# A diffusion block on one core: the first up-projection weights split ahead of the norms, modulation columns paced anew, a PSUM bank for each output of a last block

## The chip, the cores and the metric

The kernel runs on one core of one Trainium2 chip. The metric is the device time of one execution in microseconds (us); it is the median of several runs. The profile is of one further execution, whose own time stands in the table below.

## The reference, cut to what matters

The program is a backbone of two layers over 256 latent tokens and 256 context tokens, of width 2048, in fp32.

- Layer 0: the conditioning vectors give six modulation vectors (shift, scale, gate, twice) by a 2048 x 12288 product. The normalised, modulated tokens go through one input projection into query latents (512), key/value latents (256), a rotary key (64) and a pooling input (1024). The latents are normalised again and projected up to 8 heads (queries 128 + 64 rotary, keys 128 + the shared rotary key, values 128). The latent tokens attend to context and latent tokens. The pooling input goes through centred means of four widths and a small product. Attention and pooling outputs are concatenated into one output projection, with a gated residual. Then an MLP of 8192 hidden channels with a squared ReLU, again modulated, normalised and gated.
- Layer 1: modulated tokens go through a two-dimensional Fourier transform in 4 channel groups, an output projection with a gated residual, and an MLP as before.
- At the end there is a last RMS norm with its own weight.

```
p = h @ w_in
q = rmsnorm(p[:, :512], q_norm) @ w_uq
kv = rmsnorm(p[:, 512:768], kv_norm) @ w_ukv
x = x + g1 * (concat(attend(q, kv), pool(p[:, 832:])) @ w_out)
x = x + g2 * (square(relu(modulate(rmsnorm(x), sh2, sc2) @ w_mlp1)) @ w_mlp2)
```

## The kernel before, in words

**Precision.** Every large fp32 operand is split into a high part (a cast to fp32r on ScalarE, ACT) and a low part (the difference, on VectorE, DVE); TensorE (PE) multiplies high by high, high by low and low by high. `split` (L131) does this for 128 x 1024 elements of a weight tile, into a tile of tag H and one of tag L, six of each (L52). A weight tile W is 128 x 2048 (1 MB), comes in by one DMA on SyncE (SP) in `load` (L121), and has six buffers (L51). PSUM has eight banks (L57).

**Modulation columns.** For the vectors of layer 0 behind the first two, and for all of layer 1, each 128 columns of the modulation weight are one W tile: DVE multiplies it with the broadcast conditioning and sums it, in one instruction (L103). These tiles wait in a list `todo`. `load` adds `pace[0]` to a counter for each weight that it loads and lets as many columns follow on SP as the counter has whole ones; their sums are issued with the next load (`mod_sums`). `mod_rest` issues what is left. In the mixer of layer 0, 48 columns (gate, scale and shift: `mod_vector(0, 2)`, `(0, 4)`, `(0, 3)`) are due before the MLP's norm.

**Order.** SP and PE run in the order of the program text (`manual_schedule`, L49); the instructions of ACT and DVE are put in an order by the compiler's list scheduler, which mostly keeps the text's and may pull ready work forward. All queues are in order when they run.

**The stages around the change.** A loop over 8 groups computes modulation of the first norm, the latents and the first half of the pooling input. Then `weave(attention(), pooling())` (L725) interleaves two generators: when `attention` yields n, n half steps of `pooling` run on PE before it goes on.

- `attention` (L580): squares of the latents, token sums, `rstd` and `spread` (yield 1, yield 1), the normalised latents and their splits, the shared key's rotary part and its split (yield 2), then `project(0)` for the first pair of heads (yield 1), `scores` (yield 2), and for each head `turned` (transposes of the softmax), for odd heads `project` of the next pair (yield 1), `scores` of the next head, `values`, yield 2. `project` loads and splits the pair's key/value weight (512 KB, one split) and query weight (768 KB, two splits) itself.
- `pooling` (L525): four weight tiles of the second half of the pooling input, in two half steps each; copies out of PSUM with a yield of their own; the band matmuls, the small product, and then the pooling half of the output projection in 16 half steps. 29 half steps in all.

When both are done, four `linear` calls (L728) do the attention half of the output projection in eight loads, `mod_rest` runs, and `renorm` (L300) forms the norm of the MLP; its waking matmuls (`awake`, tile `wk`) keep PE busy meanwhile.

**Output blocks.** `linear` (L183) accumulates four output blocks of 128 channels at a time. With `slim`, two blocks share a bank, each a half of it, and they are evacuated together when the second is done. With `drain`, both half steps of the last weight are done block by block. Both are set in the last group of four of the even projection, of each MLP and of the odd projection. The evacuation is `residual` (L500): a gated update of x on DVE, its square on ACT, and the sum of squares on DVE, for the last two blocks (LATE) left to PE. The very last MLP also scales x by the final norm's weight (L521).

Lines that the prediction's steps touch: L103 column sum, L135 and L136 split, L242 sum of squares, L268 waking matmuls, L512 update, L519 and L521 late square and final scaling, L638 to L644 rotary query, L675 row maximum of the scores, L691 and L694 transposes and their copies.

Of the kernel before, what the change touches and what calls it, by code (L numbers as in the profile page):

```python
# [19 lines left out]
NB = D // P  # L20
# [23 lines left out]
def hybrid_dit(ctx: ExitStack, tc: tile.TileContext, xT, ctxT, c2, cb_in, vecs, wmod_s, wmod0, wmod1,  # L44
# [32 lines left out]
    def half(b, i):  # L77
        return b[:, i * T:(i + 1) * T]
# [42 lines left out]
    def load(src, n=2048):  # L121
        mod_sums()
        w = wp.tile([P, 2048], F32, name="W", tag="W")
        nc.sync.dma_start(w[:, :n], src)
        pace[1] += pace[0]
        while pace[1] >= 1 and todo:
            pace[1] -= 1
            mod_step()
        return w
# [13 lines left out]
    def split_pair(h, l, src):  # L143
        nc.scalar.copy(h, src)
        nc.vector.tensor_tensor(l, src, h.bitcast(F32), ALU.subtract)
# [21 lines left out]
    def narrow(o, wts, j, acts, first, last):  # L167

        js = slice(j * P, (j + 1) * P)
        n = len(wts)  # L170
        for k, (h, l) in enumerate(wts):
            mm(o, h[:, js], acts[k][:, :T], first and k == 0, False)
            mm(o, h[:, js], acts[k][:, T:], False, False)
            mm(o, l[:, js], acts[k][:, :T], False, last and k == n - 1)
# [8 lines left out]
    def linear(tiles, acts, evac, nb=4, slim=False, drain=False):  # L183


        if slim:
            banks = [bank() for _ in range(nb // 2)]
            ps = [half(banks[j // 2], j % 2) for j in range(nb)]
        else:
            ps = [bank() for _ in range(nb)]  # L190
        for i, (srcs, k0) in enumerate(tiles):
            for s, src in enumerate(srcs):
                w = load(src)
                final = i == len(tiles) - 1
                for k in (0, 2):
                    wts = split(w, k * 512, 1024, 512)
                    first, last = i == 0 and k == 0, final and k == 2
                    part = acts[k0 + k:k0 + k + 2]
                    if drain and final:
                        if k == 0:  # L200
                            held = wts
                            yield
                            continue
                        wts, part = held + wts, acts[k0:k0 + 4]
                    elif not slim:
                        wides(ps[4 * s:4 * s + 4], wts, part, first, last,
                              lambda j: evac(4 * s + j, ps[4 * s + j]))
                        yield
                        continue
                    for j in range(4):  # L210
                        o = ps[4 * s + j]
                        if slim:
                            narrow(o, wts, j, part, first and j % 2 == 0, last and j % 2 == 1)
                        else:
                            wide(o, wts, j, part, first, last)

                        if last and not slim:
                            evac(4 * s + j, o)
                        elif last and j % 2:
                            evac(4 * s + j - 1, ps[4 * s + j - 1])  # L220
                            evac(4 * s + j, o)
                    yield
# [108 lines left out]
    def column(i):  # L331
        return vec[:, i:i + 1]
# [153 lines left out]
    ropet = funit("ropet")  # L486
    nc.sync.dma_start(ropet.rearrange("p (a b) -> p a b", b=T), rope)
    bandt = [funit(f"band{i}") for i in range(4)]
    for i in range(4):
        nc.sync.dma_start(bandt[i], band[:, i])  # L490

    mod_vector(0, 2)
    mod_vector(0, 4, V_N2[0])
    mod_vector(0, 3)
    pace[0] = 1.75


    mixed = []
# [1 line left out]
    def residual(l, which, stats, slim=False):  # L500

        def at(ng):
            def evac(j, ps):
                i = 4 * ng + j
                if (l, which) not in whole:
                    mod_sums()
                assert (l, which) in whole
                g = mods[l][:, which, i:i + 1]
                if not slim:
                    t = scr("rt")  # L510
                    nc.scalar.mul(t, half(ps, 1), g)  # L511
                nc.vector.scalar_tensor_tensor(x[:, i], ps[:, :T], g, x[:, i], ALU.mult, ALU.add)  # L512
                if not slim:
                    nc.vector.tensor_tensor(x[:, i], x[:, i], t, ALU.add)  # L514
                if stats is not None and i < NB - LATE:
                    sumsq(stats[0], x[:, i], i == 0)
                elif stats is not None:
                    stats.append(scr("late"))
                    nc.scalar.square(stats[-1], x[:, i])  # L519
                if stats is not None and (l, which) == (1, 5):  # L520
                    nc.scalar.mul(x[:, i], x[:, i], column(V_FN + i))  # L521
            return evac
        return at

    def pooling():  # L525

        ut = [[funit("ut") for hf in range(2)] for tb in range(2)]
        for tb in range(2):
            nc.scalar.copy(ut[tb][0], pu0[tb])
        us = [bank(f"pu{tb}") for tb in range(2)]  # L530
        for kt in range(4):
            w = load(w_pl[1, kt])
            for i in range(2):
                for n, (h, l) in enumerate(split(w, 1024 * i, 1024, 512)):
                    by_token(us, 4 * kt + 2 * i + n, h, l)
                yield
        for tb in range(2):
            nc.scalar.copy(ut[tb][1], us[tb])
        yield
        pooled = []  # L540
        for g in range(4):
            ps = bank("pl")
            for j in range(2):
                fs = slice((g % 2) * T + j * P, (g % 2) * T + (j + 1) * P)
                for tb in range(2):
                    mm(half(ps, j), ut[tb][g // 2][:, fs], half(bandt[g], tb), j == 0 and tb == 0, j == 1 and tb == 1)
            pooled.append(funit("pl"))
            nc.scalar.copy(pooled[g], ps)
            if g % 2:
                yield  # L550
        w = load(w_pool)
        for g in range(4):
            ps = bank("po")
            for j in range(2):
                plain(half(ps, j), [w[:, k * 256:(k + 1) * 256] for k in (2 * g, 2 * g + 1)], j,
                      [half(pooled[g], 0), half(pooled[g], 1)], j == 0, j == 1)
            for j in range(2):
                u = unit("mx")
                sc, o = column(V_PS + 2 * g + j), half(ps, j)
                nc.scalar.mul(u[:, :T], o, sc)  # L560
                nc.vector.scalar_tensor_tensor(u[:, T:], o, sc, u.bitcast(F32)[:, :T], ALU.mult, ALU.subtract)
                mixed.append(u)
            if g % 2:
                yield
        for ng in range(4):
            yield from linear([((w_oe[ng, kt],), 4 * kt - 8) for kt in (2, 3)], mixed,
                              residual(0, 2, None, True)(ng), 4, True)

# [3 lines left out]
    def rotary(s):  # L572

        r = scr("rot")
        nc.vector.stream_shuffle(r, s, list(range(16, 32)) + list(range(16)))
        nc.vector.tensor_tensor(s, s, half(ropet, 0), ALU.mult)
        nc.vector.tensor_tensor(r, r, half(ropet, 1), ALU.mult)
        nc.vector.tensor_tensor(s, s, r, ALU.add)

    def attention():  # L580
        squares = []
        for b in ka[:2] + qa:
            squares.append(funit("lq"))
# [26 lines left out]
            split_act(ql[j], f)  # L610
        kr = funit("kr")
        nc.scalar.copy(kr, ka[2])
        rotary(half(kr, 1))
        krh, krl = unit("krh"), unit("krl")
        split_pair(krh, krl, kr)
        yield 2

        def project(pr):

            w = load(w_ukv[pr], 1024)  # L620
            wkv = split(w, 0, 1024, 512)
            kn, vt = [], []
            for j in range(2):
                js = slice(j * P, (j + 1) * P)
# [5 lines left out]
                    mm(ps, l[:, js], kvh[k], False, k == 1)  # L630
                kn.append((unit("knh"), unit("knl")))
                split_pair(*kn[j], ps)
            w = load(w_uq[pr], 1536)
            wuq = split(w, 0, 768, 384) + split(w, 768, 768, 384)
            ps = bank("qr")
            narrow(half(ps, 0), wuq, 2, ql, True, True)
            f = scr("qr")
# [67 lines left out]
            split_act(a, o)  # L705
            attn.append(a)

        pair = project(0)
        yield 1
        p = scores((pair, 0))  # L710
        yield 2
        for h in range(NH):
            us = turned(p)
            head = (pair, h % 2)
            if h < NH - 1:
                if h % 2:
                    pair = project(h // 2 + 1)
                    yield 1
                p = scores((pair, (h + 1) % 2))
            else:  # L720
                yield 1
            values(head, us)
            yield 2
# [160 lines left out]
    mod_vector(1, 5)  # L884
    acc = [stat("acc3")]
    mlp(1, h, acc, ((9, 0.0), (999, 1.7)))
    r = spread(rstd_of(acc))
    for i in range(0, NB, 2):
        o = funit("o").rearrange("p (a b) -> p a b", b=T)
        nc.vector.tensor_tensor(o, x[:, i:i + 2], r[:, None, :].to_broadcast([P, 2, T]), ALU.mult)  # L890
# [90 lines left out]
```

## Time and profile before

| | before |
|---|---|
| median of 3 runs | 1984.27 us (1983.85 to 1984.52) |
| the profiled execution | 1986.23 us |
| its span, first to last instruction | 1984.5 us |
| PE matmul busy | 1932.1 us, 97% |
| PE weight loads busy | 1707.2 us, 86% |
| DVE busy | 1459.6 us, 74% |
| ACT busy | 1016.6 us, 51% |
| mean granted TensorE clock | 0.991 of full speed |
| column sums, L103 | 160, 364.8 us of DVE |

A share over the whole span averages stages with different limits, so the rows below are of stretches. Times in them are in us from the start of the span. The row of a window gives its length, then the busy time and the count of instructions of each engine, the granted clock as a share of full speed, the busy share of the 16 DMA engines and their GB/s. A row of the timeline gives start, duration, engine, line, operation, output tile and input tiles, shape and count, and in brackets the idle time of the engine just before with what ended it. PEld is the weight load of PE. SPq is the SP queue that issues DMAs; a long duration there is a wait for a buffer.

### The profile page before, as it was taken

The page shows a single profiled execution, that of the slowest core. Times are in us where ns is not written, and L with a number is a line of the kernel's source. Part 1 is how long each engine was busy: PE and PEld are TensorE (multiplying, and loading weights), DVE is VectorE, ACT ScalarE, POOL GpSimd, SP SyncE. Part 2 cuts the span into 40 slices and gives each one's busy share as a digit, 9 for nine tenths or more (in the row PEclk, how much of TensorE's full clock was granted, in tenths as well). Part 3 has the DMA queues.
Part 4 walks back from the last instruction along what each step waited for, and adds up shares of the span by engine and source line. Part 5 has one row for each costly group of instructions (what it writes and reads, how often), then busy time and mean ns, then how long its engine had stood idle before and what let it go on. Part 6 is the DMA issues. An engine that isn't in the chain of part 4 may idle for free.

```text
span 1984.5 us, 29715 instructions
## 1 busy us (share of the span) xinstructions
PE 1932.1 (97%) x11886; PEld 1707.2 (86%) x11886; DVE 1459.6 (74%) x2042; ACT 1016.6 (51%) x1655; POOL 1.2 (0%) x13
## 2 busy tenths in 40 slices
PE   5997999999999999999999999999999999999997
PEld 4786899988888888888888989888888888888887
DVE  4448999998888888888888677897655555555564
ACT  4344654455545644644554454555456446545663
POOL 0000000000000000000000000000000000000000
PEclk9998999999999999999999999999999999999998
DMA  9997899879889879888888347598555555555541
GB/s 379 394 391 256 323 347 348 332 269 371 317 332 345 325 309 345 327 336 315 312 323 318 128 168 260 199 382 306 189 186 185 187 190 190 191 191 191 186 155 43
DMA packets 77468, 537.72 MB, mean 271 GB/s; under 512 B 8849, under 2 KB 9105, under 8 KB 14481
## 3 DMA queue, kind: packets, MB, share of 16 engines
q1 hardware_dynamic: 77328, 535.82, 72.8%
q8 instruction: 93, 1.52, 0.3%
q14 instruction: 47, 0.38, 0.1%
HBM read 533.69 MB, written 2.10 MB: 270 GB/s over the span
## 4 chain that ended last, share of the span: by engine, by line
PE 93%; DVE 4%; DMA 1%; issue 1%; ACT 1%; SPq 0%; DVEq 0%; ACTq 0%
PE mm L81 81%; PE ka L81 2%; DVE W L103 2%; PE mrow L81 2%; PE pu L81 1%; PE f L81 1%; PE qa L81 1%; PE sc L81 1%; DVE L L136 1%; DMA W<-in_wmod_s 1%; PE pv L81 1%; PE p L81 1%; PE var L81 0%; PE wk L81 0%; PE pl L81 0%
## 5 line engine op out<-in xcount | busy, mean ns | idle before, releaser
L136 DVE TENSOR_TENSOR L<-W,H 128x1024 fp32r<-128x1024 f32 (+1 forms) x620 | 743.3, 1214 | 331.8 <-ACT H L135 331.1
L135 ACT CAST H<-W 128x1024 fp32r<-128x1024 f32 (+1 forms) x620 | 638.1, 1044 | 519.3 <-PE mm L81 472.6
L81 PE MATMUL mm<-hid,H 128*128 128x512 f32 (+1 forms) x2176 | 526.9, 379 | 0.0
L81 PE MATMUL mm<-h,H 128*128 128x512 f32 x2048 | 513.2, 392 | 0.0
L81 PEld LDWEIGHTS mm<-hid,H 128*128 128x128 f32 x2176 | 385.3, 189 | 61.7
L81 PEld LDWEIGHTS mm<-h,H 128*128 128x128 f32 x2048 | 368.3, 189 | 66.8 <-DVE h L292 0.5
L103 DVE SCALAR_TENSOR_TENSOR W<-W,cb 128x2048 f32<-128x2048 f32 x160 | 364.8, 2282 | 0.3 <-DMA W<-in_wmod 0.3
L81 PE MATMUL mm<-hid,L 128*128 128x256 f32 x2048 | 303.9, 282 | 0.0
L81 PEld LDWEIGHTS mm<-hid,L 128*128 128x128 f32 x2048 | 286.5, 190 | 18.7
L81 PEld LDWEIGHTS mm<-h,L 128*128 128x128 f32 x2048 | 279.4, 190 | 19.9
L81 PE MATMUL mm<-h,L 128*128 128x256 f32 x2048 | 285.6, 282 | 0.0
L512 DVE SCALAR_TENSOR_TENSOR x<-mm,mods,x 128x256 f32<-128x256 f32 x176 | 78.2, 476 | 51.4 <-ACT rt L511 31.2
L511 ACT ACTIVATE rt<-mm,mods 128x256 f32<-128x256 f32 x132 | 53.9, 470 | 64.1 <-PE mm L81 64.1
L747 ACT COPY b<-mm 128x256 f32<-128x256 f32 x128 | 45.8, 358 | 69.7 <-PE mm L81 69.7
L750 ACT ACTIVATE rl<-g 128x256 f32<-128x256 f32 x128 | 53.2, 416 | 54.5 <-DVE g L748 53.3
L748 DVE TENSOR_TENSOR g<-mm,b 128x256 f32<-128x256 f32 x128 | 53.5, 418 | 25.9 <-ACT b L747 25.7
L81 PE MATMUL mm<-fr,H 128*128 128x512 f32 (+1 forms) x320 | 71.2, 349 | 0.0
L81 PEld LDWEIGHTS mm<-fr,H 128*128 128x128 f32 x320 | 54.5, 190 | 6.2
L751 ACT ACTIVATE hd<-rl 128x256 f32<-128x256 f32 x128 | 53.3, 416 | 2.5
L141 DVE TENSOR_TENSOR hid<-hd,hid 128x256 fp32r<-128x256 f32 x128 | 53.6, 419 | 0.3
L140 ACT CAST hid<-hd 128x256 fp32r<-128x256 f32 x128 | 52.2, 407 | 1.0
L514 DVE TENSOR_TENSOR x<-x,rt 128x256 f32<-128x256 f32 x132 | 50.9, 417 | 0.7
(223 smaller groups left out, 1558.1 us busy)
## 6 DMA issues: line engine op xcount, KB each, us to landing
W<-in_w SPq DMA_DIRECT2D x256, 1024.0 KB, 5.3
W<-in_wmod SPq DMA_DIRECT2D x160, 1024.0 KB, 6.2
W<-in_wmod_s SPq DMA_DIRECT2D x32, 1024.0 KB, 9.6
W<-in_w_oe SPq DMA_DIRECT2D x16, 1024.0 KB, 6.7
W<-in_w_oo SPq DMA_DIRECT2D x16, 1024.0 KB, 5.0
W<-in_w_pl SPq DMA_DIRECT2D x8, 1024.0 KB, 8.4
W<-in_w_kq SPq DMA_DIRECT2D x8, 896.0 KB, 9.2
W<-in_w_uq SPq DMA_DIRECT2D x4, 768.0 KB, 4.6
```

Source lines behind the costliest of these rows:

```text
L81: nc.tensor.matmul(o, l, r, start=start, stop=stop, skip_group_check=True)
L103: nc.vector.scalar_tensor_tensor(w, w, 1.0, cb, ALU.mult, ALU.mult, accum_out=mods[l][:, which, j:j + 1])
L135: nc.scalar.copy(h[:, :n], w[:, lo:lo + n])
L136: nc.vector.tensor_tensor(l[:, :n], w[:, lo:lo + n], h.bitcast(F32)[:, :n], ALU.subtract)
L140: nc.scalar.copy(u[:, :n], src)
L141: nc.vector.tensor_tensor(u[:, n:2 * n], src, u.bitcast(F32)[:, :n], ALU.subtract)
L511: nc.scalar.mul(t, half(ps, 1), g)
L512: nc.vector.scalar_tensor_tensor(x[:, i], ps[:, :T], g, x[:, i], ALU.mult, ALU.add)
L514: nc.vector.tensor_tensor(x[:, i], x[:, i], t, ALU.add)
L748: nc.vector.tensor_tensor(s, half(ps, 0), b, ALU.add)
L750: nc.scalar.activation(r, s, AF.Relu)
L751: nc.scalar.square(f, r)
```

## The change

- **Early weights.** A new function `pair_weights` loads and splits both weights of a pair of heads. For the first pair it is called at the start of `attention`, ahead of the squares and norms; for the others at the start of an odd head, ahead of `turned`. `project` takes the split tiles from a list.
- **Rotary key behind the projection.** The rotary part of the shared key and its split are issued behind `project(0)`.
- **Yields.** After each `project`, 2 half steps of the filler run instead of 1; the yield of its own behind the copies in `pooling` is gone.
- **Bands.** The four 256 KB loads of the band tables are issued one by one behind the four pooling weights instead of ahead of the weave.
- **Paces.** 1.75 columns for each load from the first load on become none for the first three loads (the pair's weights and the first pooling weight), 2.2 from there to the first group of four of the pooling half's output projection, and 1.6 from its second group on.
- **A bank for each last block.** Where `slim` and `drain` are both set, each of the four outputs gets its own bank and is evacuated at once when its matmuls end.
- **Final scaling.** For the last two blocks the scaling by the final norm's weight is issued behind the last norm's `rstd_of`.

```
-        if slim:
+        own = slim and drain
+        if own:
+            ps = [half(bank(), 0) for _ in range(nb)]
+        elif slim:
...
-                            narrow(o, wts, j, part, first and j % 2 == 0, last and j % 2 == 1)
+                            narrow(o, wts, j, part, first and (own or j % 2 == 0), last and (own or j % 2 == 1))
...
-                        if last and not slim:
+                        if last and (own or not slim):
                             evac(4 * s + j, o)
...
     bandt = [funit(f"band{i}") for i in range(4)]
-    for i in range(4):
-        nc.sync.dma_start(bandt[i], band[:, i])
...
-    pace[0] = 1.75
...
-                if stats is not None and (l, which) == (1, 5):
+                if stats is not None and (l, which) == (1, 5) and i < NB - LATE:
                     nc.scalar.mul(x[:, i], x[:, i], column(V_FN + i))
...
             w = load(w_pl[1, kt])
+            pace[0] = 2.2
             for i in range(2):
...
                 yield
+            nc.sync.dma_start(bandt[kt], band[:, kt])
         for tb in range(2):
             nc.scalar.copy(ut[tb][1], us[tb])
-        yield
...
         for ng in range(4):
+            if ng:
+                pace[0] = 1.6
             yield from linear([((w_oe[ng, kt],), 4 * kt - 8) for kt in (2, 3)], mixed,
...
+    def pair_weights(pr):
+        w = load(w_ukv[pr], 1024)
+        wkv = split(w, 0, 1024, 512)
+        w = load(w_uq[pr], 1536)
+        return wkv, split(w, 0, 768, 384) + split(w, 768, 768, 384)
+
     def attention():
+        ready = [pair_weights(0)]
         squares = []
...
-        rotary(half(kr, 1))
         krh, krl = unit("krh"), unit("krl")
-        split_pair(krh, krl, kr)
         yield 2
 
-        def project(pr):
+        def project():
-            w = load(w_ukv[pr], 1024)
-            wkv = split(w, 0, 1024, 512)
+            wkv, wuq = ready.pop()
...
-            w = load(w_uq[pr], 1536)
-            wuq = split(w, 0, 768, 384) + split(w, 768, 768, 384)
...
-        pair = project(0)
-        yield 1
+        pair = project()
+        rotary(half(kr, 1))
+        split_pair(krh, krl, kr)
+        yield 2
         p = scores((pair, 0))
         yield 2
         for h in range(NH):
+            if h % 2 and h < NH - 1:
+                ready.append(pair_weights(h // 2 + 1))
             us = turned(p)
             head = (pair, h % 2)
             if h < NH - 1:
                 if h % 2:
-                    pair = project(h // 2 + 1)
-                    yield 1
+                    pair = project()
+                    yield 2
...
-    r = spread(rstd_of(acc))
+    r = rstd_of(acc)
+    for i in range(NB - LATE, NB):
+        nc.scalar.mul(x[:, i], x[:, i], column(V_FN + i))
+    r = spread(r)
```

## Rows read from the trace of the kernel before

**Rows 1.** Windows over the mixer of layer 0: length, then busy time by engine.

```profile
166.00:218.00 52.00, 39.20 (x199) 33.01 (x199) 51.15 (x74) 26.62 (x47) 0.00 (x0) 0.93 0.85 315
180.00:190.00 10.00, 6.08 (x36) 6.08 (x37) 10.00 (x14) 4.74 (x7) 0.00 (x0) 0.66 0.95 360
218.00:254.00 36.00, 36.00 (x208) 32.44 (x208) 32.33 (x53) 21.78 (x43) 0.00 (x0) 1.00 0.84 316
254.00:330.00 76.00, 73.70 (x522) 68.72 (x520) 74.25 (x111) 42.15 (x72) 0.00 (x0) 1.00 0.93 343
330.00:392.50 62.50, 61.22 (x498) 60.19 (x496) 58.50 (x78) 24.55 (x34) 0.00 (x0) 1.00 0.92 349
```

**Rows 2.** Waits of PE, 138 to 218 us, then 218 to 330 us.

```profile
PE qr L81 <- DVE L L136: 5.3, 1, 5.3
PE kn L81 <- DVE L L136: 3.5, 1, 3.5
...
PE sc L81 <- DVE qnl L145: 2.2, 2, 1.3
```

**Rows 3.** Timeline of DVE, 138 to 222 us, and one row of ACT.

```profile
148.40 2.36 DVE L136 TENSOR_TENSOR L<-W,H 128x1024 fp32r<-128x1024 f32 x2 [7.38 <-ACT H L135]
...
176.35 2.28 DVE L103 SCALAR_TENSOR_TENSOR W<-W,cb 128x2048 f32<-128x2048 f32 x1
...
182.92 1.81 DVE L136 TENSOR_TENSOR L<-W,H 128x768 fp32r<-128x768 f32 x2
...
145.37 1.09 ACT L584 ACTIVATE lq<-ka 128x512 f32<-128x512 f32 x2 [3.48 <-PE ka L81]
```

**Rows 4.** Timeline of SP, 110 to 420 us: issues of loads.

```profile
123.00 3.45 SPq L490 DMA_DIRECT2D band<-in_band  x4
...
141.04 0.33 SPq L124 DMA_DIRECT2D W<-in_w_ukv  x1
...
162.36 0.33 SPq L124 DMA_DIRECT2D W<-in_w_uq  x1
...
366.72 0.33 SPq L124 DMA_DIRECT2D W<-in_w_oe  x1
371.83 23.36 SPq L124 DMA_DIRECT2D W<-in_w  x8
```

**Rows 5.** The page's costliest groups: the column sums.

```profile
L103 DVE SCALAR_TENSOR_TENSOR W<-W,cb 128x2048 f32<-128x2048 f32 x160 | 364.8, 2282 | 0.3 <-DMA W<-in_wmod 0.3
```

**Rows 6.** The chain that ended last: start, length, what (the MLP of layer 0 begins).

```profile
401.48 716.13 PE mm L81 x4160
```

**Rows 7.** Timeline of PE, then of ACT, at the last head's transposes.

```profile
327.20 1.03 PE L691 MATMUL tr<-ident,p 128*128 128x128 f32 x8
...
328.23 1.07 ACT L694 COPY pu<-tr 128x512 f32<-128x512 f32 x2
```

**Rows 8.** Timeline of DVE and PE behind the even projection; PE's in layer 1.

```profile
392.89 0.41 DVE L242 TENSOR_TENSOR acc<-acc,q 128x256 f32<-128x256 f32 x1
...
393.36 0.61 PE L81 MATMUL var<-ones,acc 128*128 128x1 f32 x4 [0.91 <-DVE acc L242]
...
395.86 2.72 PE L81 MATMUL wk<-at 128*128 128x512 f32 x6
...
1250.04 1.63 PE L81 MATMUL wk<-fr 128*128 128x512 f32 x6
```

**Rows 9.** Timeline of PE behind the odd projection.

```profile
1251.94 0.68 PE L81 MATMUL rb<-dg,one 128*128 128x128 f32 x4 [0.27 <-DVE dg L283]
```

**Rows 10.** Timeline of DVE, ACT and PE at the end of the program.

```profile
1970.61 0.88 DVE L512 SCALAR_TENSOR_TENSOR x<-mm,mods,x 128x256 f32<-128x256 f32 x2 [0.64 <-PE mm L81]
...
1971.57 0.51 ACT L521 ACTIVATE x<-x,vec 128x256 f32<-128x256 f32 x1
1971.99 0.40 ACT L519 ACTIVATE late<-x 128x256 f32<-128x256 f32 x1
...
1972.44 0.61 PE L81 MATMUL var<-ones,late 128*128 128x1 f32 x4 [0.24 <-ACT late L519]
```

## The prediction

> **What bounds the kernel now.** I read the busy time by stretches first, then who the matmul engine (PE) waits for, then the order of single instructions around those waits. The reader should see two things. From 166 to 218 us PE is busy 39.20 of 52.00 us, 12.80 us idle, while VectorE (DVE) is busy 51.15: DVE is full exactly where PE waits [rows 1]. From 218 to 392.5 PE is nearly full: 36.00 of 36, 73.70 of 76, 61.22 of 62.5, and DVE is at 32.33, 74.25 and 58.50. Over 166 to 392.5 DVE is busy 216.23 of 226.5 us, 95.5%. So this half of layer 0 has two bounds within a few per cent of each other, and a wait taken from PE is only kept as far as DVE has the time.
>
> The waits are single ones: the first up-projection waits 3.5 us for the low part of its first weight and its rotary query 5.3 us for that of the second [rows 2]. The timeline says why. DVE stands idle 7.38 us up to 148.40, yet the low parts of the query weights come at 182.92, behind modulation columns such as the one at 176.35 [rows 3]. The loads say the same: SP issues the keys' weight at 141.04, but the queries' weight only at 162.36, 21 us apart, since SP has to wait for one of six weight buffers and the columns loaded on the way hold them until DVE has summed them [rows 4].
>
> **The early weights.** Each of the first pair's weights moves ahead of the norms, its DMA, casts and subtractions with it. On SP they pass four band transfers (3.45 us of issue from 123.00, [rows 4]), which go behind pooling loads, and the first two pooling weights; these are used only behind the loop's last pooling inputs, and I cost that at nothing, with the one subtraction more that then stands ahead of them (1.2 us) as the other end. On DVE one subtraction of 1024 elements (half of the 2.36 us of two at 148.40) and two of 768 (1.81 us) leave the full stretch for the idle 7.38 us [rows 3]: 3.0 us of DVE work less. On ACT the three casts wait for their DMAs with the latents' squares queued behind them, and PE's token sums wait for those; ACT had 3.48 us idle ahead of the squares [rows 3], which takes up the casts, and PE has two pooling inputs and a half step to do before the sums: nothing. With the splits both PE waits of rows 2, 8.8 us, lose their cause. The next thing due there is the low half of the second normalised key latent; kr's rotary and split are behind the projection, and two pooling half steps of matmuls instead of one stand ahead of the first scores, so that this is not late. For the later pairs the loads keep their place on SP; on ACT their casts pass the copies of `turned`, which are needed only behind `project` and `scores`: nothing.
>
> **The columns.** A column costs DVE 2.28 us [rows 5], and 48 are due before the norm of the MLP in either kernel. By the paces, before issued 1, 3, 5, 7 with its first four loads; after has 0, 0, 0, 2. At load 21, the last ahead of the eight attention loads of the output projection, it is 36 before and 34 after; the last load ends at 48 before and at 47 after. The 48th then goes out alone behind the last output weight (366.72), ahead of the MLP's first weight (371.83) [rows 4], which is used from 401.48 [rows 6]: nothing, with 2.28 us as the other end. So columns are not saved, they are put off by 5 (11.4 us of DVE), then caught up with.
>
> **What of it stays.** The DVE work of 166 to 392.5 becomes 216.23 - 3.0 = 213.2 us. At the share of 95.5% that DVE has now this takes 223.3 us, a gain of 3.2; at the 97.7% of 254 to 330, the best of the long stretches, 218.2 us, a gain of 8.3. The nearest rows are these two, on either side; the columns that stood in the way now have DVE time with nobody waiting, but there is less of it later, so I take the middle, **5.7 us**. Below 3.2 nothing excludes a loss, since the later stretches have only 3.67 + 1.75 + 4.00 = 9.4 us of DVE idle for 11.4 us of deferred columns; above, PE alone would allow the 12.80 us, and about 2 us of the 6.08 busy in 180 to 190, where the granted clock averaged 0.66 between its two levels of 1.2 and 2.4 GHz [rows 1]: 14.8 us.
>
> **The steps given away.** Each later projection is followed by two half steps of filler instead of one, which covers the 2.2 us in which scores waited for a query split [rows 2]. The filler has 28 half steps (29 before) and the attention takes 31 (27): it ends three yields early. So the last head's values follow its transposes at once. PE's transposes ended at 328.23 and the two copies out of PSUM at 329.30 [rows 7]: 1.07 us uncovered, twice that if a cast comes first. While DVE is the bound these two only move PE's idle time about; both are inside the 5.7.
>
> **A bank per last block.** In the three drained blocks (and the one that ends layer 0's MLP) each of the four outputs gets its bank and is evacuated when its matmuls end, not two by two. The same instructions run. After the even projection PE waited 0.91 us for a sum that DVE had queued behind the evacuation of block 14, which its shared bank held up to the last matmul, and then six waking matmuls took 2.72 us there against 1.63 in the other norm [rows 8]. I take **0.9 us**, between 0 and 2.0 (0.9 and the 1.09 of slower matmuls). In the odd projection PE is filled with waking matmuls and waits 0.27 us [rows 9]: **0.2**, between 0 and 0.3. After layer 0's MLP the Fourier matmuls start with the first channels, not the last: 0, between -0.3 and 0.3, as that nearest row. At the very end nothing covers: block 15's square came at 1971.99, behind block 14's square and final scaling, and the variance matmul at 1972.44. With block 14 out early and the two scalings behind the variance, block 15's update takes about half of the 0.88 us of two from 1970.61, its square 0.40, and the matmul can come at about 1971.5 [rows 10]: **0.9 us**, between 0.4 (only the 0.51 us scaling goes) and 1.0. Extra banks can only cost if one is late; those of the blocks before have the whole of the last blocks' matmuls to be evacuated in.
>
> **Sum.** The profiled execution took 1986.23 us (span 1984.5). 1986.23 - 5.7 - 0.9 - 0.2 - 0.9 = 1978.5. It was 1.96 us above the median of 1984.27, so the median forecast is 1976.6 us.
>
> **Rivals.**
> First, **PE gets it all back**: DVE finds room for the put-off columns because PE's queue runs less jerkily. Then 14.8 us, the 2.2 of rows 2 less the 1.07 of rows 7, and the 2.0 of the blocks are kept: 17.9, a time of 1966.4. For it speaks that PE is at 98% in 330 to 392.5 and DVE at 94%; against it, that only 9.4 us of DVE idle are left behind 218 us. The Trainium skill (Perfetto Trace Analysis, Identifying the Most-Contended Engine) takes the engine of highest occupancy as the bound, and for TensorE the weight loads' share, not the matmuls'. By that rule, 60.19 us of weight loads against 58.50 of DVE in 330 to 392.5 name PE there, which would favour this rival; in 166 to 218 they name DVE (33.01 against 51.15), as the trace agrees. Chance 0.15.
>
> Second, **DVE keeps what PE gains**, or the edits do not arrive: the program fixes the order of SP and PE alone, so columns may be put among the norms again, and the early casts may wait for one of six split buffers that the last latents hold. Then only the blocks' 2.0 us stay: 1982.3. For it speaks that DVE has no idle time from 166 to 218. Chance 0.21.
>
> Third, **slower: a backlog at the end**. The last eight loads bring 14 columns, not 12: 22 transfers of 1.05 MB against 20, 23.1 against 21.0 MB. At the 349 GB/s of 330 to 392.5 that is 66.1 us against 60.1, in a stretch in which SP already waits for buffers; DVE has 4.00 us idle for two more columns of 2.28. PE would then wait up to 6.0 us for output weights behind columns, and 2.1 for the last head. With the low end of the early gain and the blocks: 1984.27 - 3.2 - 2.0 + 8.1 = 1987.2, and up to 1990.4 without the early gain. It decides if the loads of the output projection do not run ahead of PE. The Trainium skill (Perfetto Trace Analysis, Roofline) puts a single core's ceiling at about 435 GB/s; an estimate by that page is 53 us for the 23.1 MB, and no wait, but no stretch of rows 1 shows such a rate. Chance 0.09.
>
> **How the numbers follow.** The forecast has 0.55, and by its bounds 1972 to 1981. The range from 1966.5 to 1984 leaves out about half of the first rival, the third, and little else. A measurement tells about 0.2%, 4.0 us, from no change: faster is below 1980.3, slower above 1988.2. The forecast gives 0.52 to faster and 0.03 to the same; with the first rival faster has 0.67. The second gives 0.21 to the same; the third is split, 0.03 and 0.06. So 0.67, 0.27, 0.06.
>
> **What would show it.** Right: the idle 12.80 us of PE from the norms to the second pair gone or under 4, the query weights' low parts before 150 us, the variance matmul at the end 0.9 us earlier against the last matmul. Wrong: PE waiting for weights or buffers in the output projection by more than 5 us (third), or the MLP starting within 2 us of 401.5 with the early waits gone (second), or over 12 us before it (first).

## The result and the profile after

The changed kernel takes **2012.08 us** (median of 4 runs, 2010.15 to 2013.36) against 1984.39 us for the kernel before (4 runs beside them): a ratio of **1.0135, interval 1.0122 to 1.0148**. The forecast was 1976.6 us, faster. It is slower by 27 us, and outside the range.

The profiled execution took 2012.43 us (span 2010.4). The loss lies in one place. Layer 0's MLP starts 25.6 us late: the first fence has PE's first matmuls of it in after, the second those in before. (After's chain runs without a break only from 439.32 us, where [rows 6] have 401.48, but that is 56 matmuls into the MLP, behind a wait of 1.65 us for DVE.) The MLP ends at 1145.16 us instead of 1117.61, 27.5 us late; everything behind that takes 865.2 us, before 866.9.

```profile
427.00 2.29 PE L81 MATMUL mm<-h,H 128*128 128x512 f32 x8
```

```profile
401.39 2.28 PE L81 MATMUL mm<-h,H 128*128 128x512 f32 x8
```

The cause starts earlier. First the busy time by stretches of after, in the columns of [rows 1].

```profile
138.00:166.00 28.00, 26.20 (x158) 23.16 (x156) 12.17 (x28) 14.93 (x21) 0.00 (x0) 0.94 0.33 125
166.00:218.00 52.00, 39.07 (x171) 31.72 (x172) 33.13 (x51) 17.85 (x31) 0.00 (x0) 0.84 0.63 241
218.00:254.00 36.00, 32.80 (x172) 28.96 (x171) 28.83 (x42) 18.47 (x35) 0.00 (x0) 0.95 0.69 257
254.00:330.00 76.00, 70.08 (x475) 65.34 (x474) 71.15 (x104) 36.60 (x65) 0.00 (x0) 0.96 0.89 331
330.00:392.50 62.50, 59.27 (x446) 56.59 (x445) 59.09 (x84) 29.27 (x48) 0.00 (x0) 1.00 0.89 337
```

DVE, full from 166 to 218 us before (51.15 of 52.00), is busy 33.13 there; the DMA share falls from 0.85 to 0.63, and from 0.68 to 0.33 in the stretch ahead. Over all five stretches DVE is busy 204.37 us, before 230.98: **26.6 us of DVE work not done by 392.5**, about as much as the MLP's end is late. The work is then done late: the sums of three columns (6.6 us of L103) stand on the chain that ended last between 405 and 418 us. PE is busy 9.8 us less (227.41 against 237.18). So nothing became busier; DVE was starved early, in a part of the program where it was nearly full before.

What starved it stands in SP's waits, 115 to 240 us (waiter, releaser: total, times, longest), and in SP's timeline.

```profile
SPq L538 <- PE pu L81: 28.5, 1, 28.5
...
SPq L538 <- DVE krl L145: 12.7, 1, 12.7
...
SPq L538 <- DVE h L295: 8.9, 1, 8.9
SPq L538 <- PE sc L81: 8.8, 1, 8.8
...
SPq L538 <- PE ka L81: 7.3, 1, 7.3
```

```profile
126.13 0.33 SPq L124 DMA_DIRECT2D W<-in_w_uq  x1
129.83 0.33 SPq L124 DMA_DIRECT2D W<-in_w_pl  x1
146.36 0.33 SPq L538 DMA_DIRECT2D band<-in_band  x1
146.74 0.42 SPq L124 DMA_DIRECT2D W<-in_w_pl  x1
147.22 0.90 SPq L96 DMA_DIRECT2D W<-in_wmod  x2
176.67 0.33 SPq L538 DMA_DIRECT2D band<-in_band  x1
177.09 0.38 SPq L124 DMA_DIRECT2D W<-in_w_pl  x1
177.56 0.86 SPq L96 DMA_DIRECT2D W<-in_wmod  x2
191.16 0.33 SPq L538 DMA_DIRECT2D band<-in_band  x1
...
201.80 0.33 SPq L538 DMA_DIRECT2D band<-in_band  x1
202.23 0.38 SPq L124 DMA_DIRECT2D W<-in_w_ukv  x1
```

L538 is the band transfer. All four wait, 66.2 us together (the first waits 16.2 us, for h and then for ka; the expectations below count 57.3, without the 8.9 for h). Each time the next pooling weight, or at last the second pair's key/value weight, and two columns stand behind it on SP and go out within 2 us of its release. From 148.1 to 176.67 SP issues nothing. By the kernel's text the band tiles share the 36 activation buffers, and the releasers are instructions that read or write activation tiles, so I read the waits as waits for a buffer. Ahead of the weave, in the kernel before, all four bands went out within 3.45 us [rows 4]. The DMA view of 140 to 215 us, in 40 slices (the row gives the busy share in tenths), shows the empty pipe in after; the second fence is the same row of the kernel before (21.52 MB, after 14.85 MB).

```profile
DMA  0000999960000000000099997002899956999999
```

```profile
DMA  9999407992005984037989997999699569799999
```

The PE side: the waits of the first pair's projections [rows 2] are gone (what is left for qr belongs to later pairs, the first at 235.30 us), and the pooling input waits for casts instead (PE, 138 to 392 us).

```profile
PE pu L81 <- ACT H L135: 12.1, 3, 6.0
PE qr L81 <- DVE L L136: 4.0, 2, 2.2
PE mm L81 <- DVE L L136: 3.2, 4, 1.8
```

The longest of these is not a wait for a load. The second pooling weight was issued at 146.74, and such a load lands 5.9 us later (median), yet ACT casts it at 170.07, behind the copy of kr, and only then does PE go on. These same pooling matmuls are what the second band waits for (PE pu, up to 176.67), and the third pooling weight stands behind that band. So the late cast lengthens the wait on SP:

```profile
169.60 0.57 ACT L622 COPY kr<-ka 128x512 f32<-128x512 f32 x1
170.07 1.99 ACT L135 CAST H<-W 128x1024 fp32r<-128x1024 f32 x2
171.17 0.80 PE L81 MATMUL pu<-H,h 128*128 128x512 f32 x1 [6.04 <-ACT H L135]
```

The order of ACT is the compiler's; with the bands on another queue (experiment 4) the same text gets these casts at 151.82 and 154.06, among the norms:

```profile
151.82 1.05 ACT L135 CAST H<-W 128x1024 fp32r<-128x1024 f32 x1
```

The other parts of the change did arrive. The first pair's low parts are made by 146.1 us (before, the query weight's: 182.92, [rows 3]), and at the end of the program the variance follows the last matmul's end (1997.88) by 1.01 us, before 1.86 [rows 10]:

```profile
143.13 2.96 DVE L136 TENSOR_TENSOR L<-W,H 128x1024 fp32r<-128x1024 f32 x3 [1.83 <-ACT H L135]
```

```profile
1989.95 7.93 PE mm L81 x66
...
1997.91 0.50 DVE x L512
...
1998.42 0.42 ACT late L519
...
1998.89 0.62 PE var L81 x4
```

### The profile page after: what moved, and what is told of

Its sections match the earlier page's. It is cut to its first block, busy times and chain, and to the rows that moved or that the text cites. A ratio compares the mean times of both kernels' runs of the same rounds, so it can differ in the third digit from the quotient of the medians.

```text
span 2010.4 us, 29695 instructions
## 1 busy us (share of the span) xinstructions
PE 1943.2 (97%) x11886; PEld 1715.2 (85%) x11886; DVE 1461.4 (73%) x2042; ACT 1015.3 (51%) x1655; POOL 1.2 (0%) x13
## 4 chain that ended last, share of the span: by engine, by line
PE 92%; DVE 5%; DMA 1%; issue 1%; ACT 1%; SPq 0%; DVEq 0%; ACTq 0%
PE mm L81 78%; PE pu L81 2%; PE ka L81 2%; DVE W L103 2%; PE mrow L81 1%; PE f L81 1%; PE sc L81 1%; DVE L L136 1%; PE qa L81 1%; DMA W<-in_wmod_s 1%; PE pv L81 1%; PE p L81 1%; PE qn L81 1%; PE v L81 0%; PE var L81 0%
## 5 line engine op out<-in xcount | busy, mean ns | idle before, releaser
L103 DVE SCALAR_TENSOR_TENSOR W<-W,cb 128x2048 f32<-128x2048 f32 x160 | 364.6, 2283 | 0.4 <-DMA W<-in_wmod 0.4
L81 PE MATMUL pu<-H,h 128*128 128x512 f32 x128 | 47.1, 438 | 12.1 <-ACT H L135 12.1
```

The source lines that it names most:

```text
L81: nc.tensor.matmul(o, l, r, start=start, stop=stop, skip_group_check=True)
L103: nc.vector.scalar_tensor_tensor(w, w, 1.0, cb, ALU.mult, ALU.mult, accum_out=mods[l][:, which, j:j + 1])
```

## The experiments

The theory: the band loads, waiting on SP for a buffer, hold up the loads behind them, and DVE is starved. Rival A: the new paces and yields do it (columns put off into a stretch that has no DVE time for them). Rival B: the early weights do it, by holding split buffers. A third is the extra banks. All kernels compute the whole reference. Ratios are to the kernel before, timed beside each.

**1. After, with the bands ahead of the weave again, on SP.**

```
     bandt = [funit(f"band{i}") for i in range(4)]
+    for i in range(4):
+        nc.sync.dma_start(bandt[i], band[:, i])
...
-            nc.sync.dma_start(bandt[kt], band[:, kt])
```

> The changed kernel with the four band loads put back ahead of the weave, nothing else. Theory (each band load waits on SP for an activation buffer, and the pooling weight and columns queued behind it on SP wait too): the band waits of 28.5, 12.7, 8.8 and 7.3 us go, PE no longer waits for pooling casts (12.1 us before), DVE is busy over 45 of the 52 us from 166 to 218 instead of 33, and the time is 1976 to 1984 us. Rival A (the new paces put the columns off, and DVE lacks time later): 2003 to 2012 us, DVE still idle early. Rival B (the early weights hold three of the six split buffers and the pooling casts wait for those): PE keeps 8 to 12 us of waits for casts, 1995 to 2010 us.

Measured: 1982.23 us, ratio 0.9985 (0.9976 to 0.9995). The loss is gone, with all other parts of the change in place. DVE is busy again:

```profile
166.00:218.00 52.00, 47.81 (x243) 40.37 (x242) 50.55 (x87) 26.07 (x48) 0.00 (x0) 0.95 0.76 295
```

But only 3 us of the prediction's 7.7 are there. The first pair's last query casts come at 148.2, against 143.65 in experiment 4: behind the bands' 1 MB, SP issues the query weight at 131.25 us, there at 125.63.

**2. Before, with the band loads alone moved behind the pooling weights.**

```
-    for i in range(4):
-        nc.sync.dma_start(bandt[i], band[:, i])
...
+            nc.sync.dma_start(bandt[kt], band[:, kt])
```

> The kernel before with only the four band loads moved behind the pooling weights. Theory (band loads block SP): 1995 to 2012 us, with band waits of over 40 us in all on SP. Rival A (paces) and rival B (split buffers): within 3 us of before, 1982 to 1987 us.

Measured: 2009.42 us, ratio 1.0125 (1.0111 to 1.0139): this one move makes nearly the whole loss. Its SP waits (L535 is the band transfer there) and PE's:

```profile
SPq L535 <- PE pu L81: 47.3, 2, 28.0
```

```profile
PE pu L81 <- ACT H L135: 11.6, 3, 8.7
```

**3. Before, with the banks and the late scaling alone.**

```
+        own = slim and drain
+        if own:
+            ps = [half(bank(), 0) for _ in range(nb)]
-        if slim:
+        elif slim:
...
+    for i in range(NB - LATE, NB):
+        nc.scalar.mul(x[:, i], x[:, i], column(V_FN + i))
```

> The kernel before with only a bank for each last block and the final scaling of the last two blocks put late. By the terms of the prediction 2.0 us less than before (0.9 behind the even projection, 0.2 behind the odd, 0.9 at the end): 1982.3 us, between 1980.8 and 1983.8. If after the even projection nothing is saved, because DVE is late there for other reasons: 1983.2 us. From the trace of the changed kernel, whose part behind the first MLP is 1.6 us shorter than before, a gain under 1.0 us would speak against all of it.

Measured: 1983.86 us, ratio 0.9991 (0.9983 to 1.0000): 1.8 us by the ratio, 2.0 had been summed, and the interval reaches to nothing, so the banks are neither the cause of the loss nor a sure gain. Behind the even projection PE waits 0.61 us (0.91 before), and its waking matmuls take 1.65 (2.72 before, [rows 8]):

```profile
391.81 0.61 PE L81 MATMUL var<-ones,acc 128*128 128x1 f32 x4 [0.61 <-DVE acc L245]
```

**4. After, with the same band loads at the same place issued by GpSimd (POOL).**

```
-            nc.sync.dma_start(bandt[kt], band[:, kt])
+            nc.gpsimd.dma_start(bandt[kt], band[:, kt])
```

> The changed kernel with the band loads at their new places, but issued from GpSimd's queue instead of SP's. Theory (it is the queue that is blocked, not the bands that are late): within 4 us of the version with the bands ahead, and over 15 us faster than the changed kernel. If the bands themselves come too late for their matmuls, or the buffers that they take delay others: within 5 us of the changed kernel, 2005 to 2015 us. Rivals A and B: 2005 to 2015 us too.

Measured: **1974.98 us**, ratio 0.9952 (0.9938 to 0.9965), 37 us under the changed kernel by one word. It is also 6.5 us (by the ratios) under the kernel with the bands ahead, where a difference of at most 4 was expected; experiment 7 takes that up. The bands still wait (POOL's timeline), with nothing behind them, and PE and DVE are both nearly full:

```profile
146.15 0.67 POOL L538 DMA_DIRECT2D band<-in_band  x1 [144.39 <-PE ka L81]
170.74 0.54 POOL L538 DMA_DIRECT2D band<-in_band  x1 [23.92 <-PE pu L81]
183.39 0.54 POOL L538 DMA_DIRECT2D band<-in_band  x1 [12.11 <-DVE qrl L649]
189.51 0.54 POOL L538 DMA_DIRECT2D band<-in_band  x1 [5.58 <-PE sc L81]
```

```profile
166.00:218.00 52.00, 49.23 (x254) 41.80 (x253) 48.30 (x73) 28.55 (x52) 1.61 (x3) 0.97 0.82 314
```

So it is not that the bands come late, but what stands behind them: they are issued at 146.15 to 189.51 us here, at 146.36 to 201.80 in after, and in after their first matmul comes only at 220.9. The Trainium skill (DMA: Bandwidth & Descriptors, Issuing engines are not separate DMA queues) says that starting transfers on several engines saves only the time that a sequencer takes to start them. Where a transfer waits for its buffer that is not so here: 0.33 us of issue each, and 37 us of time, with the order of ACT that came with the other queue in it.

**5. Experiment 4 with the old pace**, 1.75 columns from the first load on.

```
     mod_vector(0, 3)
+    pace[0] = 1.75
...
-            pace[0] = 2.2
...
-            if ng:
-                pace[0] = 1.6
```

> The changed kernel with the bands on GpSimd's queue (1975.0 us), and the paces of before: 1.75 columns a load from the first load on. If putting the columns off helps, as the prediction has it, because fewer of them stand among the norms: 1979 to 1985 us, with column sums again ahead of the latents' splits and 2 to 8 us more of PE waits from 154 to 218. Rival (the paces do nothing, since the early weights alone remove the waits; a steadier pace even leaves less to catch up with in the output projection): 1972 to 1977 us.

Measured: 1978.76 us, ratio 0.9967 (0.9955 to 0.9979): the new paces are worth some 3 us where the weights are early (the intervals overlap); the time lies between the two ranges expected. PE stalls early again (24.13 us busy from 138 to 166, 26.99 in experiment 4), while DVE sums columns for 11.39 us there (4.58 in experiment 4).

**6. Experiment 4 with each pair's weights loaded in front of its projection.**

```
-        ready = [pair_weights(0)]
+        ready = []
...
+        ready.append(pair_weights(0))
         pair = project()
...
-            if h % 2 and h < NH - 1:
-                ready.append(pair_weights(h // 2 + 1))
...
                 if h % 2:
+                    ready.append(pair_weights(h // 2 + 1))
                     pair = project()
```

> The changed kernel with the bands on GpSimd's queue, and each pair's weights loaded and split in front of its projection again, as before (the columns then come one or two loads earlier in the first loads). By the prediction the early weights are worth most of the gain: 1979 to 1986 us, PE waiting 3 to 9 us for the low parts of the first pair's weights. Rival (the paces alone remove those waits, since no column stands ahead of the splits): 1973 to 1977 us.

Measured: 1980.58 us, ratio 0.9978 (0.9969 to 0.9987): with the new paces, the early weights and what goes with them are worth 5.2 us (0.0026 of 1984.4). The edit brings the columns forward too: by 218 us DVE has summed 36.3 us of them, in experiment 4 29.6, and two columns forward cost some 3 us by themselves (experiment 12). How much of the 5.2 us is the weights alone is not shown.

**7. Before, with the bands behind the pooling weights, on GpSimd.** The edit is that of experiment 2, with `nc.gpsimd`.

> The kernel before with only the band loads moved behind the pooling weights and issued from GpSimd's queue. If the gain of that queue is that SP is not blocked and nothing else: 1982 to 1987 us, the time of before. If the bands' 1 MB and 3.45 us of SP time ahead of the pooling weights cost before something, as the 7 us between the two versions of the changed kernel suggest: 1976 to 1981 us.

Measured: 1978.93 us, ratio 0.9969 (0.9958 to 0.9981). Moved without SP's queue, the bands alone gain 6.2 us. SP issues the first query weight at 153.93 instead of 162.36 [rows 4], and the waits of [rows 2] shrink from 8.8 us to 1.4 with no weight early:

```profile
PE qr L81 <- DVE L L136: 0.8, 2, 0.6
...
PE kn L81 <- DVE kvl L145: 0.6, 1, 0.6
```

**8. After, with all four bands on SP behind the fourth pooling weight.**

```
-            nc.sync.dma_start(bandt[kt], band[:, kt])
+        for i in range(4):
+            nc.sync.dma_start(bandt[i], band[:, i])
```

> The changed kernel with all four band loads on SP, but behind the fourth pooling weight and its columns instead of one behind each. By the theory of the blocked queue only the second pair's weights queue behind them: the band waits on SP fall from 57 us to under 25, the pooling weights come in time, and the time is 1976 to 1988 us. If any wait of a band on SP costs its length: 1990 to 2005 us.

Measured: 1993.02 us, ratio 1.0039 (1.0025 to 1.0054), not the theory's 1976 to 1988 but in the second range. The pooling weights are now ahead of the bands, ACT casts the second one at 151.94 us, as in experiment 4, and PE is as busy as there (48.81 of 52). One wait of 22.3 us still holds up columns and the second pair's weights; DVE does 9.7 us less there, and that is paid later:

```profile
SPq L539 <- PE pu L81: 23.3, 2, 22.3
```

```profile
166.00:218.00 52.00, 48.81 (x255) 42.49 (x254) 38.62 (x67) 26.25 (x49) 0.00 (x0) 0.95 0.57 216
```

This is the clearest case of the mechanism: no late cast and no stall of PE to be seen where the fault is, and 18 us more than experiment 4.

**9 to 11. Building the change up without SP's wait.** Experiment 9 is 7 with the banks of 3. Experiment 10 adds the early weights to 9, with the old paces, yields and rotary part. Experiment 11 is experiment 4 with the old yields and rotary part, that is 10 with the new paces. The first fence is part of 10 against 9, the second part of 11 against the changed kernel.

```
+        ready = [pair_weights(0)]
...
-        pair = project(0)
+        pair = project()
```

```
+        rotary(half(kr, 1))
         krh, krl = unit("krh"), unit("krl")
+        split_pair(krh, krl, kr)
...
         pair = project()
-        rotary(half(kr, 1))
-        split_pair(krh, krl, kr)
-        yield 2
+        yield 1
```

> The kernel before with two parts only: the bands on GpSimd's queue behind the pooling weights, and a bank for each last block with the late scaling. If the two gains add (6.2 and 1.8 us alone): 1976.3 us, ratio 0.996, and early weights, paces, rotary key and yields together are then worth 1.5 us in the best version so far (0.9952). If they don't add, since a mixer that ends earlier has DVE late behind the even projection: 1978 to 1979 us, and the other parts are worth 3 to 4 us.

> The version with bands on GpSimd's queue and banks, with the early weights added, and nothing else of the change (old paces, old places of the rotary key and of the yields). By the prediction's step for the early weights (3.2 to 8.3 us): 1968 to 1973 us. By its second rival (DVE is full and keeps what PE gains; g1 with the old paces showed 1978.8): 1975 to 1980 us.

> The changed kernel with the bands on GpSimd's queue (0.9952), with the rotary key ahead of the projection and the yields as before. By the prediction both only move PE's idle time about: 1973 to 1977 us. If covering the query split with a second half step matters: 1978 to 1981 us. If the uncovered last head costs more than that: 1970 to 1973 us.

Measured: 1977.86 us, ratio 0.9965 (0.9953 to 0.9978); 1980.16 us, 0.9970 (0.9958 to 0.9982); **1974.51 us, 0.9947 (0.9934 to 0.9961)**, the best of all. The gains of 7 and 3 add within the intervals (0.9960 if they do). The early weights by themselves add nothing to 9, where the prediction's step would have brought 3.2 to 8.3 us; with the paces they bring 3.6 us over 9 (0.9965 to 0.9947, intervals that overlap). The new yields and the rotary part's place make no difference that these runs can tell (0.9952 against 0.9947).

**12. Experiment 4 with the columns one load earlier.**

```
-            w = load(w_pl[1, kt])
             pace[0] = 2.2
+            w = load(w_pl[1, kt])
```

> The changed kernel with the bands on GpSimd's queue, and 2.2 columns already with the first pooling weight, so that the last load ends at 48 and none is left for the end. If DVE's idle time from 138 to 166 us is the resource that decides (each column summed there is one less in the output projection): 1971 to 1974 us, with two columns more ahead of 166 us. If those two columns only delay the pooling weights' splits, as with the old paces: 1976 to 1979 us.

Measured: 1978.65 us, ratio 0.9966 (0.9954 to 0.9978). Two columns earlier cost some 3 us (intervals that overlap a little); which wait that is was not followed.

**13 and 14. Would more activation buffers cure it?** After, and before, with 40 activation buffers for 36, and five weight buffers for six to make room.

```
-    wp = ctx.enter_context(tc.tile_pool(name="wp", bufs=6))
+    wp = ctx.enter_context(tc.tile_pool(name="wp", bufs=5))
-    ap = ctx.enter_context(tc.tile_pool(name="ap", bufs=36))
+    ap = ctx.enter_context(tc.tile_pool(name="ap", bufs=40))
```

> The changed kernel with 40 activation buffers instead of 36, paid for with five weight buffers instead of six. If what a band load waits for on SP is a free activation buffer: the band waits on SP fall from 57 us to under 25, and although a weight buffer is missing the time falls to 1985 to 2000 us. If it is something else (a semaphore of an earlier load, the order of SP): the waits stay over 45 us and the time is 2010 to 2025 us.

> The kernel before with the same 40 activation and five weight buffers, to price the missing weight buffer. SP waits for weight buffers all through the mixer, so 2 to 12 us slower than before: 1986 to 1996 us; if six are more than it needs, within 2 us of before.

Measured: 2026.34 us, ratio 1.0205 (1.0188 to 1.0222); 1991.85 us, 1.0029 (1.0019 to 1.0040). The band waits fall from 66.2 to 33.1 us, but the loss against a kernel before with the same buffers grows to 34 us. Both ranges expected failed. One wait of 24 us is left at the place of the 28.5:

```profile
SPq L96 <- DVE L L136: 51.3, 6, 16.0
SPq L538 <- DVE kvl L145: 23.9, 1, 23.9
...
SPq L538 <- PE pu L81: 3.9, 2, 2.9
SPq L538 <- PE ka L81: 3.7, 1, 3.7
SPq L538 <- DVE h L295: 1.6, 1, 1.6
```

The columns (L96) wait 51.3 us for weight buffers besides, in after 15.7, so the missing one mixes in. The releasers change with the number of buffers (kvl here, in after pu), but that a free one would end the waits is not shown. Nor is the load all of it: here the second pooling weight was issued 8 us earlier than in after (138.36 us), and ACT still casts it at 173.13. So what of after's 27 us is the wait on SP itself and what the order of ACT that came with it stays open. Experiment 8 has the wait without the late cast, and is 18 us slower than experiment 4.

## Why the prediction was wrong, point by point

**The step that failed** is in the early weights: bands "go behind pooling loads ... I cost that at nothing". It counted SP's 3.45 us in front of the weights (1.7 of them a wait of SP for an earlier DMA) and saw that what the weights pass is used only later. It did not ask what a band moved behind pooling loads has to wait for, nor what is queued behind it then. That was 66.2 us of waits on SP and, alone, +1.25% or 25 us (experiment 2); from experiment 4 to after it is 37 us. How much of these is the wait on SP alone and how much ACT's late casts stays open; without late casts it was 18 us (experiment 8 against 4). The prediction had read such a wait in [rows 4], of SP for weight buffers, with work queued behind.

Of the prediction's own signs two came true in after (the low parts by 146.1 us, the end 0.85 us earlier). The first sign did not: from 166 to 218 us PE was idle 12.93 us, before 12.80; in experiment 4 it was 2.77.

**The bound** fits the size: DVE was 95.5% busy from 166 to 392.5 us in before, and the columns not summed when they were due (6 by 218 us, before 14, counting from 138 at 2.28 us each) were not made up. The DVE time from 138 to 392.5 us against that of before gives the large results roughly: -26.6 us in after (+27 measured), -21.5 in experiment 2 (+25), -10.0 in experiment 8 (+8). It doesn't order the small ones: experiments 9 and 11 differ by 1.1 us in it, and 3.6 us in time.

**The rivals.** None named the wait. The third, slower by a backlog of columns in the output projection, had the way in which it is paid, but put the cause in the paces. The second, that the early weights gain nothing, holds for the early weights alone (experiment 10).

**The early weights, 5.7 us (3.2 to 8.3).** In the range where the paces come with them and the bands' queue is out of the way (5.2 us, experiment 6, with columns brought forward mixed in); nothing with the old paces (experiment 10). The waits of [rows 2] did not need early weights to go: taking the bands from SP alone leaves 1.4 of the 8.8 us (experiment 7). The prediction saw only the columns in them.

**The steps given away and the yields**: no difference that experiment 11 can tell, as costed. **The columns**, "put off by 5 ..., then caught up with": caught up with they were, without SP's wait (109.45 us of sums from 138 to 392.5 in experiment 4, before 109.57); put off they were less, by one column at 218 us (29.61 us against 31.72).

**The blocks, 0.9 + 0.2 + 0.9 us.** The end of the program gave 0.85 us and the odd projection 0.1 (0.16 us of wait, before 0.27, [rows 9]); the even projection gave 0.3 of wait and 1.1 of waking matmuls by itself (experiment 3), and nothing in after, where DVE is late there (0.98 us of wait).

The sum, 1976.6 us, lies within 2 us of experiment 4 (1974.98). That is partly luck: the bands' going, which the sum put at nothing, is worth 6.2 us by itself (experiment 7), and the early weights, to which it gave 5.7, nothing that experiment 10 can tell without the paces.

## What to carry to other kernels

A transfer that can wait for its destination's buffer belongs on a queue with nothing urgent behind it; before one is moved, ask which buffer it gets, who frees that and when, and what is queued behind. Where an engine is over 95% busy for a long stretch, expect time lost to starvation there to stay lost, as it did here; the wait that shows it can be on a queue and not on any compute engine. Prices of parts that share a cause (early weights, paces, bands) don't add; try them in the order in which they would be built up.

## What was not expected of the hardware

A band transfer on GpSimd, with nothing behind it, waited 23.92 us in the fastest kernel but one, where on SP such a wait was part of 37 us. The granted clock fell with the starving, 0.84 from 166 to 218 us in after and 0.81 in experiment 2, against 0.93 before and 0.97 in experiment 4, a mean between its levels of 1.2 and 2.4 GHz, behind PE's waits of up to 6.04 us (after) and 8.7 us (experiment 2). And taking 1 MB of band tables and their 3.45 us on SP from ahead of the loads gained 6.2 us (experiment 7); which of the two it was is not shown.
